# Low parts of weights by an accumulating SBUF transfer instead of a VectorE subtraction, in the middle of a hybrid decoder trunk

## The chip, the cores and the metric

The kernel runs on one core of a Trainium2 chip. A core has a matrix engine (TensorE, PE in the profile, with its weight loads shown apart as PEld), a vector engine (VectorE, DVE), an engine for pointwise functions (ScalarE, ACT), a programmable engine (GpSimd, POOL) and a queue engine (SyncE, SP). Data comes through 16 DMA engines, which SP, ACT and POOL can all start. The engines run side by side, each through its own instructions in order, and wait for each other by semaphores.

The metric is the device time of one execution in microseconds, as the median of the runs.

## The reference

Two layers, on 512 tokens of width 1024, all in float32. Each layer norms its input and projects it once into the inputs of three branches and three gates:

```python
xn = rmsnorm(x, norm1_g)
proj = xn @ w_in
...
y_ssd = ssd_mixer(...)          # Mamba-2: conv, chunked scan over 4 chunks of 128, gated norm
y_mla = mla_mixer(...)          # latent attention, 8 heads, causal
y_gdn = gdn_mixer(...)          # gated DeltaNet: conv, triangular solves, chunked scan
mixed = g_ssd * (y_ssd @ w_ssd_out) + g_mla * (y_mla @ w_mla_out) + g_gdn * (y_gdn @ w_gdn_out)
h = x + mixed @ w_out
f = jnp.square(jax.nn.relu(rmsnorm(h, norm2_g) @ w_up)) @ w_down
return h + f
```

The output is the norm of the second layer's result. Almost all of the arithmetic is in products of the 512 tokens with weight matrices that are read once.

## The kernel before

**Two-part arithmetic.** Every large product is made of three products of rounded numbers. A weight `w` is split into a high part, `w` rounded to the type float32r, and a low part, `w` minus the high part; activations likewise. `mm3` (L179) adds high x high, high x low and low x high in PSUM.

**How weights come in.** `weights` (L164) walks down a matrix. `weights_raw` (L157) loads 128 x 1024 float32 (512 KB) through SP's queue into a tile `wraw`, of which there are two buffers. Each such tile is split in two pieces of 128 x 512 by `split_half` (L148): ScalarE's copy rounds the piece into `whi` (L153), and VectorE subtracts it from the raw piece into `wlo` (L154). `whi` and `wlo` have four buffers each. `dense_F` (L185) and `dense_T` (L217) then issue twelve matmuls for each piece. A raw buffer can be loaded again when both of its pieces have been split; a `whi` or `wlo` buffer can be written again when the last matmul that reads it is done.

**The order of a layer.** First the small projections, the latents and attention (L353 to L660). Then, in a pool `br`, the part that the change concerns (L1038 to L1061): `ssd_group` twice (L685), each with projections, a convolution and a scan of four chunks; `gdn_decays` (L782), which loads and computes decay matrices and stores them; the output projection of attention, in two halves between these; `gdn_matrix` twice (L790) and `gdn_blocks` (L832), a chain of 62 small VectorE operations; the output projection of the state-space branch with the steps of `gdn_inverse` between its blocks; `gdn_unit` twice (L927), each with projections and a scan of four chunks; and the output projection of the gated-delta branch. `out_proj` (L462) also projects the gate of its branch. After that come `w_out` with the residual, and the feed-forward part.

**What sets the order.** A scheduler lays out each engine's instructions from the program and from priorities. The split of weights stands under a high priority, so that it goes ahead of other work on ScalarE and VectorE as soon as its buffers are free. POOL has little to do: it raises small tiles to the powers that norms need (`rsq`, L263, and L809, L939) and clears some tiles. The decay matrices `eE` are loaded through SP's queue, the same as the weights (L455, L820, L967).

Of the kernel before, what the change touches and what calls it, by code (L numbers as in the profile page):

```python
# [15 lines left out]
ALU = mybir.AluOpType  # L16
# [38 lines left out]
def hybrid_kernel(ctx, tc, a, out, depth=2, taps=None):  # L55
    nc = tc.nc
    pe, act, dve, pool, sync = nc.tensor, nc.scalar, nc.vector, nc.gpsimd, nc.sync
    uid = itertools.count()

    def mk(pl, shape, dt, tag, bufs=None):  # L60
        return pl.tile(shape, dt, tag=tag, name=f"{tag}_{next(uid)}", bufs=bufs)

    def tap(name, ap):
        if taps and name in taps:
            sync.dma_start(taps[name], ap)

    def f32(ap):
        return ap.bitcast(F32)
# [76 lines left out]
        act.activation(cosT, nn, AF.Sin)  # L145


    def split_half(raw, hold=None, first=True):  # L148

        n = raw.shape[1]  # L150
        hi, lo = hold or (mk(wp, [P, n], F32R, "whi"), mk(wp, [P, n], F32R, "wlo"))
        with tc.high_priority() if first else nullcontext():
            act.copy(hi, raw)  # L153
            dve.tensor_tensor(lo, raw, f32(hi), ALU.subtract)  # L154
        return hi, lo

    def weights_raw(w2d, c0, n, k0, kt):  # L157

        raw = mk(wp, [P, kt * n], F32, "wraw", 2)
        sync.dma_start(raw.rearrange("p (k n) -> p k n", n=n),  # L160
                       w2d[k0 * P : (k0 + kt) * P, c0 : c0 + n].rearrange("(k p) n -> p k n", p=P))
        return raw

    def weights(w2d, c0, n, K, hold=None, raw0=None):  # L164

        kt = min(1024 // n, K // P)
        step = 512 // n  # L170
        for k0 in range(0, K // P, kt):
            given = raw0 is not None and k0 == 0
            raw = raw0 if given else weights_raw(w2d, c0, n, k0, kt)
            for q in range(0, kt, step):
                hi, lo = split_half(raw[:, q * n : (q + step) * n], hold and hold[k0 + q], not given)
                v = lambda x: x.rearrange("p (k n) -> p k n", n=n)
                yield k0 + q, v(hi), v(lo)

# [6 lines left out]
    def dense_F(gen, cols, K, xh, xl, mid=None, banks=None, after=None):  # L185

        pss = banks or [acc_bank() for _ in cols]
        last = K // P - 1
        if mid:
            gen = list(gen)
            for i, hf in enumerate(HALVES):
                for ps, c in zip(pss, cols):
                    for k0, wh, wl in gen:
                        for k in range(wh.shape[1]):
                            kk = k0 + k  # L200
                            mm3(ps[:, hf], wh[:, k, c], wl[:, k, c], xh[kk][:, hf], xl[kk][:, hf], kk == 0, kk == last)
                if i == 0:
                    mid()
            return pss
        for k0, wh, wl in gen:
            for ps, c in zip(pss, cols):
                for k in range(wh.shape[1]):
                    a_, b_ = wh[:, k, c], wl[:, k, c]
                    mm3(ps[: a_.shape[1], :], a_, b_, xh[k0 + k], xl[k0 + k], k0 + k == 0, k0 + k == last)
            if after:  # L210
                after()
        return pss

    def tiles(n):
        return [slice(i, i + P) for i in range(0, n, P)]
# [55 lines left out]
    def hilo_tags(pl, base, n=KD, w=S):  # L271
        return ([mk(pl, [P, w], F32R, f"{base}h{k}") for k in range(n)],
                [mk(pl, [P, w], F32R, f"{base}l{k}") for k in range(n)])
# [44 lines left out]
    def small_weights(raw, first=True):  # L318
        res = []
        for q in range(2):  # L320
            hold = [mk(lp, [P, 384], F32R, "mix", 8) for _ in range(2)]
            hi, lo = split_half(raw[:, q * 384 : (q + 1) * 384], hold, first)
            res.append((4 * q, hi.rearrange("p (k n) -> p k n", k=4), lo.rearrange("p (k n) -> p k n", k=4)))
        return res
# [11 lines left out]
    for t in range(T):  # L336
        if t == 2:
            params = load_params(0, False)
        ss = mk(sp, [P, 2], F32, "nss", 4)
        for i in range(2):  # L340
            if t == 2 and i == 1:

                raws0 = small_raw(0), weights_raw(a["w_in"][0], O_CQ, 512, 0, 2)
            hf = slice(i * 512, (i + 1) * 512)
            sync.dma_start(xt[:, t, hf], xsrc[t * P : (t + 1) * P, hf])
            if t == i == 1:
                jk = mk(hpl, [P, 512], F32, "hj", 2)
                dve.scalar_tensor_tensor(jk, xt[:, t, hf], 1.0, xt[:, t, hf], ALU.mult, ALU.mult, accum_out=ss[:, i : i + 1])
            else:
                square(ss[:, i : i + 1], xt[:, t, hf], hpl, "hj")  # L350
        ssq.append(ss)
    xh, xl = hilo_tags(lp, "x")
    norm_half(0, [xt[:, t] for t in range(T)], ssq, lambda k: params[0][:, 124 + k : 125 + k], hpl, xh, xl)  # L353
    for ly in range(depth):
# [24 lines left out]
        smalls(HALVES[0])  # L379
        cq_tok = [mk(lp, [P, 512], F32, "mix", 8) for t in range(T)]  # L380
        dense_T(weights(w_in, O_CQ, 512, D, raw0=None if ly else raws0[1]), 512, D, xh, xl, lambda t, ps: act.copy(cq_tok[t], ps), mid=second_half)
        h_pool.close()

# [78 lines left out]
        def out_proj(w2d, br, yh, yl, pl, part=range(4), after=None):  # L462
            for dp in part:
                tg = []
                for ps in dense_F(weights(w_in, O_GATE + br * D + dp * 256, 256, D), tiles(256), D, xh, xl, after=after):
                    t_ = mk(pl, [P, S], F32, "cva", 2)
                    act.activation(t_, ps, AF.Tanh, scale=0.5)
                    tg.append(t_)
                for j, ps in enumerate(dense_F(weights(w2d, dp * 256, 256, D), tiles(256), D, yh, yl, after=after)):
                    d = 2 * dp + j  # L470
                    if mixed[d] is None:
                        mixed[d] = mk(lp, [P, S], F32, "mix", 8)
                        dve.scalar_tensor_tensor(mixed[d], tg[j], 1.0, ps, ALU.add, ALU.mult)
                    else:
                        dve.scalar_tensor_tensor(tg[j], tg[j], 1.0, ps, ALU.add, ALU.mult)
                        dve.tensor_tensor(mixed[d], mixed[d], tg[j], ALU.add)
# [57 lines left out]
        for hp in range(4):  # L534
# [67 lines left out]
            for j in range(2):  # L602
# [3 lines left out]
                for t in range(T):  # L606
                    n = max(256, (t + 1) * P)
# [9 lines left out]
                    n = (t + 1) * P  # L617
# [10 lines left out]
                for kbs in ((0,), (1,), (3, 2)):  # L628
                    ps = sm_bank()
                    n = 0  # L630
# [296 lines left out]
        def gdn_unit(u, kT, ork, cc, cd, Yt, yh, yl):  # L927
# [102 lines left out]
            for c in range(4):  # L1030
# [4 lines left out]
                split_gain(yh[k], yl[k], ps, col(g_gdn))  # L1035
                tap(f"ygdn{k}", f32(yh[k]))

        ys = hilo_tags(lp, "y")  # L1038
        d_e = mk(dr, [2, T, P, 4, P], F32, "d_e", 2)
        ssd_group(0, *ys)  # L1040
# [17 lines left out]
        for u in range(2):  # L1058
            gdn_unit(u, *mats[u], *yg)
        out_proj(a["w_gdn_out"][ly], 2, *yg, br)  # L1060
        bp.close()  # L1061


# [13 lines left out]
        with tc.tile_pool(name="wo", bufs=1, reuse_waits="tile") as wo:  # L1077
            for c in range(2):
# [6 lines left out]
                hold = list(zip(*hilo_tags(wo, "w"))) if c == 1 else None  # L1085
# [18 lines left out]
        with tc.tile_pool(name="ff", bufs=1, reuse_waits="tile") as fp:  # L1104
# [72 lines left out]
            def down(qd, ops, b):  # L1177
# [9 lines left out]
                def product(ps, n, raw, start, i, j, op, done):  # L1187

                    w = []
                    for k in range(4):  # L1190
                        w.append(split_half(raw(k)))
                        if done == 2 and qd == 3:
                            continue
                        for t in range(2):
                            mul(ps, n, w, k, t, start)
                    for t in range(2):
                        if done == 2 and qd == 3:
                            for k in range(4):
                                mul(ps, n, w, k, t, start)
                        r = 2 * i + t  # L1200
                        hs_ = h[:, r, j * 512 : (j + 1) * 512]
                        with tc.high_priority():
                            dve.tensor_tensor(hs_, hs_, ps[t], op)
                        if done and qd == 3:
                            square(h_ssq[r][:, j : j + 1], hs_, fp, "fs", 3)
                            if done == 2:
                                finish(r, gb)
# [82 lines left out]
```

## Time and profile before

| | |
|---|---|
| median of 2 runs | 2339.37 us (2336.67 to 2342.07) |
| profiled execution, its span | 2334.6 us; no other time is given for this execution, and the two runs shown lie 2.1 and 7.5 us above it |
| TensorE busy | 2294.8 us (98%), weight loads 1891.3 us (81%) |
| VectorE busy | 1582.1 us (68%) |
| ScalarE busy | 1159.8 us (50%) |
| GpSimd busy | 58.6 us (3%) |
| moved by DMA | 240.38 MB, mean 103 GB/s |

Busy time of TensorE counts pipelined matmuls from start to a modelled end, so a busy share near 100% says that it was never long without work, not that it ran at its peak. In a row of a group the form is: line, engine, operation, what is written and read, shapes, count, then busy time in total and the mean of one in nanoseconds, then the idle time of the engine just before these instructions and what ended most of it. A row of waits gives who waited for whom, the time in total, how often, and the longest. A row of DMA issues gives tile and source, the queue, the count, the size of one, and the median time in microseconds from the issue to the landing.

### The profile page before, as it was taken

The page shows a single profiled execution, that of the slowest core. Times are in us where ns is not written, and L with a number is a line of the kernel's source. Part 1 is how long each engine was busy: PE and PEld are TensorE (multiplying, and loading weights), DVE is VectorE, ACT ScalarE, POOL GpSimd, SP SyncE. Part 2 cuts the span into 40 slices and gives each one's busy share as a digit, 9 for nine tenths or more (in the row PEclk, how much of TensorE's full clock was granted, in tenths as well). Part 3 has the DMA queues.
Part 4 walks back from the last instruction along what each step waited for, and adds up shares of the span by engine and source line. Part 5 has one row for each costly group of instructions (what it writes and reads, how often), then busy time and mean ns, then how long its engine had stood idle before and what let it go on. Part 6 is the DMA issues. An engine that isn't in the chain of part 4 may idle for free.

```text
span 2334.6 us, 32156 instructions
## 1 busy us (share of the span) xinstructions
PE 2294.8 (98%) x11926; PEld 1891.3 (81%) x11926; DVE 1582.1 (68%) x3100; ACT 1159.8 (50%) x2403; POOL 58.6 (3%) x74
## 2 busy tenths in 40 slices
PE   8999999999999999999999999999999999999998
PEld 7788787878887888888888887888788878888886
DVE  6776656875675458668767765667756645677668
ACT  6656644333443345545656557443334434545545
POOL 0000000000000000000010000000000000000000
PEclk9999999999999999999999999999999999999999
DMA  4323533352222443243132235334422224333231
GB/s 136 87 63 92 169 101 109 109 154 73 86 69 72 140 150 108 73 127 108 44 101 81 82 91 170 101 105 139 118 82 86 68 77 158 126 118 100 91 109 46
DMA packets 208221, 240.38 MB, mean 103 GB/s; under 512 B 33920, under 2 KB 155456, under 8 KB 208064
## 3 DMA queue, kind: packets, MB, share of 16 engines
q1 hardware_dynamic: 204544, 233.07, 32.7%
q10 hardware_dynamic: 3520, 5.25, 0.9%
q8 instruction: 94, 1.54, 0.3%
q14 instruction: 63, 0.52, 0.1%
HBM read 221.41 MB, written 11.63 MB: 100 GB/s over the span
## 4 chain that ended last, share of the span: by engine, by line
PE 86%; DVE 7%; DMA 3%; ACT 2%; POOL 1%; issue 1%; ACTq 0%; SPq 0%; DVEq 0%; POOLq 0%
PE acc L181 22%; PE acc L182 22%; PE acc L183 22%; PE sm L183 2%; PE sm L182 2%; PE sm L181 2%; DVE wlo L154 1%; PE sm L730 1%; DMA eE<-d_c 1%; DVE tok L846 1%; DMA mix<-mix 1%; PE sm L633 1%; DVE gQ L845 1%; PE yt L182 1%; PE sm L1003 1%
## 5 line engine op out<-in xcount | busy, mean ns | idle before, releaser
L154 DVE TENSOR_TENSOR wlo<-wraw,whi 128x512 fp32r<-128x512 f32 x552 | 378.3, 689 | 429.2 <-ACT whi L153 412.4
L153 ACT CAST whi<-wraw 128x512 fp32r<-128x512 f32 x552 | 341.4, 621 | 598.0 <-PE acc L182 371.0
L183 PE MATMUL acc<-xh,wlo 128*128 128x512 f32 (+1 forms) x1184 | 460.9, 390 | 0.0
L181 PE MATMUL acc<-xh,whi 128*128 128x512 f32 (+1 forms) x1184 | 460.7, 390 | 0.0
L182 PE MATMUL acc<-xl,whi 128*128 128x512 f32 (+1 forms) x1184 | 460.0, 389 | 0.0
L183 PEld LDWEIGHTS acc<-xh,wlo 128*128 128x128 f32 x1184 | 223.6, 189 | 41.9
L182 PEld LDWEIGHTS acc<-xl,whi 128*128 128x128 f32 x1184 | 223.5, 189 | 42.0 <-DVE xl L261 0.4
L181 PEld LDWEIGHTS acc<-xh,whi 128*128 128x128 f32 x1184 | 223.2, 189 | 41.7 <-ACT xh L260 0.4
L181 PE MATMUL acc<-yh,whi 128*128 128x512 f32 x384 | 151.9, 399 | 0.0
L182 PE MATMUL acc<-yl,whi 128*128 128x512 f32 x384 | 151.4, 394 | 0.0
L183 PE MATMUL acc<-yh,wlo 128*128 128x512 f32 x384 | 151.3, 394 | 0.0
L183 PE MATMUL acc<-whi,xl 128*128 128x512 f32 (+1 forms) x384 | 144.0, 375 | 0.0
L182 PE MATMUL acc<-wlo,xh 128*128 128x512 f32 (+1 forms) x384 | 143.9, 375 | 0.0
L181 PE MATMUL acc<-whi,xh 128*128 128x512 f32 (+1 forms) x384 | 142.6, 374 | 0.0
L674 DVE SCALAR_TENSOR_TENSOR ckl<-acc,pc,ckl 128x511 f32<-128x511 f32 (+2 forms) x168 | 120.4, 744 | 16.9 <-ACT ckl L670 8.3
L153 ACT CAST whi<-wr 128x512 fp32r<-128x512 f32 x128 | 79.5, 621 | 68.2 <-PE acc L183 32.7
L183 PE MATMUL acc<-whi,yl 128*128 128x512 f32 x256 | 99.7, 389 | 0.0
L181 PE MATMUL acc<-whi,yh 128*128 128x512 f32 x256 | 99.7, 389 | 0.0
L182 PE MATMUL acc<-wlo,yh 128*128 128x512 f32 x256 | 99.6, 389 | 0.0
L154 DVE TENSOR_TENSOR wlo<-wr,whi 128x512 fp32r<-128x512 f32 x128 | 85.8, 686 | 12.5 <-ACT whi L153 11.7
L181 PEld LDWEIGHTS acc<-yh,whi 128*128 128x128 f32 x384 | 71.7, 188 | 16.8 <-ACT yh L260 1.7
L182 PEld LDWEIGHTS acc<-yl,whi 128*128 128x128 f32 x384 | 72.2, 188 | 15.3 <-issue 1.0
(411 smaller groups left out, 4545.3 us busy)
## 6 DMA issues: line engine op xcount, KB each, us to landing
wraw<-in_w_in_dram SPq DMA_DIRECT2D x148, 512.0 KB, 3.6
wraw<-in_w_up_dram SPq DMA_DIRECT2D x64, 512.0 KB, 3.6
wr<-in_w_down_dram SPq DMA_DIRECT2D x32, 1024.0 KB, 5.0
eE<-d_c SPq DMA_DIRECT2D x48, 256.0 KB, 4.0
wraw<-in_w_mla_out_dram SPq DMA_DIRECT2D x16, 512.0 KB, 3.4
eE<-d_e SPq DMA_DIRECT2D x32, 256.0 KB, 3.0
wraw<-in_w_ssd_out_dram SPq DMA_DIRECT2D x16, 512.0 KB, 3.4
wraw<-in_w_gdn_out_dram SPq DMA_DIRECT2D x16, 512.0 KB, 3.3
```

The costliest lines, as they stand in the source:

```text
L153: act.copy(hi, raw)
L154: dve.tensor_tensor(lo, raw, f32(hi), ALU.subtract)
L181: pe.matmul(o, ah, bh, start=start, stop=False, skip_group_check=more)
L182: pe.matmul(o, ah, bl, start=False, stop=False, skip_group_check=more)
L183: pe.matmul(o, al, bh, start=False, stop=stop, skip_group_check=more)
L633: pe.transpose(ps[:, n : n + P], pn[t][:, kb * P : (kb + 1) * P], ident)
L674: dve.scalar_tensor_tensor(acc[:, d:], ps[:, : S - d], taps_[3 - d], acc[:, d:], ALU.mult, ALU.add)
L730: pe.matmul(py[:, h * 64 : (h + 1) * 64], e2[h // 4][:, h % 4, :], xd[:, h * 64 : (h + 1) * 64], start=True, stop=True)
L845: dve.tensor_tensor(pd, bc_last(nb[:, m, m + 1 :], m + 1), bc_mid(xb[:, m, : m + 1], 31 - m), ALU.mult)
L846: dve.tensor_tensor(xb[:, m + 1 :, : m + 1], xb[:, m + 1 :, : m + 1], pd, ALU.add)
L1003: pe.matmul(po[:, h * P : (h + 1) * P], pt_[:, h, :], vn[:, h * P : (h + 1) * P], start=True, stop=True)
```

## The change

In the part of each layer from the first `ssd_group` to the last `out_proj`, `split_half` makes the low part in another way. ScalarE still copies the raw piece to `whi`. Then ScalarE multiplies the raw piece by minus one into `wlo`; since `wlo` is of type float32r this is minus the high part. Then POOL starts a transfer from the raw piece to `wlo` that adds what it brings to what is there: raw minus high. Outside that part the subtraction on VectorE stays. The flag `added` chooses, and is set and cleared in the layer's code.

```diff
-    def split_half(raw, hold=None, first=True):
+    def split_half(raw, hold=None, first=True, added=False):
...
         with tc.high_priority() if first else nullcontext():
             act.copy(hi, raw)
-            dve.tensor_tensor(lo, raw, f32(hi), ALU.subtract)
+            if added:
+                act.mul(lo, raw, -1.0)
+                pool.dma_start(out=lo, in_=raw, accum_op=ALU.add)
+            else:
+                dve.tensor_tensor(lo, raw, f32(hi), ALU.subtract)
         return hi, lo
...
+    added = [False]
...
-                hi, lo = split_half(raw[:, q * n : (q + step) * n], hold and hold[k0 + q], not given)
+                hi, lo = split_half(raw[:, q * n : (q + step) * n], hold and hold[k0 + q], not given, added[0])
...
+        added[0] = True
         ys = hilo_tags(lp, "y")
...
         out_proj(a["w_gdn_out"][ly], 2, *yg, br)
+        added[0] = False
         bp.close()
```

## The prediction

> **What bounds the kernel now.** I read the page first: busy shares, the chain that ended last, and the two groups that the change touches.
>
> ```profile
> span 2334.6 us, 32156 instructions
> ...
> PE 2294.8 (98%) x11926; PEld 1891.3 (81%) x11926; DVE 1582.1 (68%) x3100; ACT 1159.8 (50%) x2403; POOL 58.6 (3%) x74
> ...
> PE 86%; DVE 7%; DMA 3%; ACT 2%; POOL 1%; issue 1%; ACTq 0%; SPq 0%; DVEq 0%; POOLq 0%
> ...
> L154 DVE TENSOR_TENSOR wlo<-wraw,whi 128x512 fp32r<-128x512 f32 x552 | 378.3, 689 | 429.2 <-ACT whi L153 412.4
> L153 ACT CAST whi<-wraw 128x512 fp32r<-128x512 f32 x552 | 341.4, 621 | 598.0 <-PE acc L182 371.0
> ```
>
> TensorE carries 86% of the chain that ends last; VectorE carries 7%. The subtraction is the costliest VectorE group, yet VectorE waits 412.4 us for the high part ahead of it, and ScalarE waits 371.0 us for TensorE ahead of the high part. The weights are therefore prepared as soon as TensorE gives a buffer back, and TensorE is what everybody waits for.
>
> Next, the two stretches of the trace that the change covers (one per layer, from the first weights of the state-space group to the last of the gated-delta output), and a dense piece of the first. The columns are busy time and instructions of each engine, the granted clock, the mean busy share of the 16 DMA engines, and what they moved.
>
> ```profile
> core 0: us, PE busy (x) PEld busy (x) DVE busy (x) ACT busy (x) POOL busy (x), PEclk, DMA share, GB/s
> 165.00:785.00 620.00, 610.94 (x3314) 498.04 (x3315) 399.60 (x830) 278.40 (x593) 19.96 (x18) 0.99 0.36 102
> 1325.00:1940.00 615.00, 608.70 (x3326) 496.70 (x3325) 399.66 (x830) 279.96 (x596) 19.96 (x18) 1.00 0.35 103
> 740.00:780.00 40.00, 40.00 (x178) 33.14 (x177) 17.86 (x28) 11.21 (x19) 0.00 (x0) 1.00 0.37 106
> ```
>
> TensorE is idle 620 - 610.94 = 9.1 us and 615 - 608.70 = 6.3 us there: 15.4 us together. That is the whole prize, whatever VectorE is spared. The waits of TensorE in the first stretch say how much of it is VectorE's (time in total, times, longest):
>
> ```profile
> PE sm L730 <- DVE eE L725: 2.5, 2, 1.4
> PE sm L879 <- DMA wk<-d_x: 1.8, 1, 1.8
> PE sm L984 <- DVE tok L981: 1.7, 4, 0.5
> PE yt L1034 <- DVE tok L1029: 1.4, 2, 0.9
> PE sm L800 <- DVE ft L269: 0.8, 1, 0.8
> PE yt L763 <- DVE tok L758: 0.6, 1, 0.6
> ```
>
> VectorE: 7.0 us of 8.8. The same share of the second layer's 6.3 is about 5, so 12 us in both. None of these is a wait for weights.
>
> **The change part by part.** A piece is 512 columns of weights, and each feeds 12 matmuls. Per layer the two state-space groups have 20 pieces each, the three output projections 32 each, the two key tiles 4 each and the two gated-delta units 20 each: 184, so 368 in both layers.
>
> *Removed:* 368 x 0.689 = 254 us of VectorE, none of it in the list of TensorE's waits. VectorE falls from 400 to 273 of 620 us in a stretch. What it can give is some of the 12 us. Those waits are for the last link of short chains, not for a queue of subtractions, so I take a third: -4 us.
>
> *Added on ScalarE:* a multiplication by minus one of the same shape and rounding as the cast, so 368 x 0.621 = 229 us, 114 per layer: 278 becomes 393 of 620 us. It fits; what matters is its place in the weights' chain.
>
> *Added on POOL and the DMA engines:* 368 transfers of 128x512 f32 (256 KB), each waiting for its multiplication. The trace before has none from POOL and none that accumulates. Rows near it, with size and median time from issue to landing:
>
> ```profile
> eE<-d_c SPq DMA_DIRECT2D x48, 256.0 KB, 4.0
> d_e<-eE SPq DMA_DIRECT2D x16, 256.0 KB, 4.1
> mix<-mix ACTq DMA_DIRECT2D x16, 128.0 KB, 2.7
> h<-hd SPq DMA_DIRECT2D x4, 512.0 KB, 6.5
> out_dram<-h SPq DMA_DIRECT2D x8, 256.0 KB, 2.0
> ```
>
> Below: 2.0 us, a plain 256 KB out of SBUF at the quiet end. Above: 6.5 us, twice the bytes. Nearest is 4.1 us, a plain 256 KB out of SBUF in this very region. To add, the engine must read the destination as well as the source. The dense piece moves 106 GB/s at a share of 0.37, hence 286 GB/s when fully busy, so one more pass over 0.262 MB is 0.9 us. I take 4.1 + 0.9 = 5.0 us and keep 2.0 and 6.5.
>
> *Moved: when a raw buffer comes free.* There are two raw buffers of two pieces each, and SyncE loads a buffer again only when both low parts are made. The dense piece shows this, by start and duration, with the time to landing of its loads:
>
> ```profile
> 753.29 0.62 ACT L153 CAST whi<-wraw 128x512 fp32r<-128x512 f32 x1 [2.05 <-PE acc L182]
> ...
> 754.12 0.69 DVE L154 TENSOR_TENSOR wlo<-wraw,whi 128x512 fp32r<-128x512 f32 x1
> ...
> 754.84 0.37 SPq L160 DMA_DIRECT2D wraw<-in_w_gdn_out_dram  x1
> 756.01 0.62 ACT L153 CAST whi<-wraw 128x512 fp32r<-128x512 f32 x1 [2.10 <-PE acc L182]
> ```
> ```profile
> DMA to landing us min/median/max: 3.2/3.5/3.8
> ```
>
> The load goes out at 754.84, as the subtraction ends at 754.81. After the change it goes out when the accumulation has landed. A buffer's round is then: load 3.5, four operations on ScalarE 4 x 0.62 = 2.5, the second transfer L, hand-overs about 0.2; in sum 6.2 + L. TensorE runs 178 matmuls in 40 us, 0.225 us each, so it eats a piece in 2.70 us and the four pieces of both buffers in 10.8 us. **The transfer is hidden up to L = 4.6 us**; beyond, each four pieces cost L - 4.6. With the four low-part buffers there is more room (a piece has 3 x 2.70 = 8.1 us for 1.2 + L, so L up to 6.9), so the raw buffers decide. At L = 5.0 that is 0.4 us for each of 92 rounds, 37 us, if all ran at the dense pace; the mean pace of a stretch is 620/184 = 3.4 us a piece, so I count between two thirds and all: 25 to 37, **+31 us**.
>
> *DMA share.* With two passes a transfer takes 1.8 us of all 16 engines. In a stretch that is 0.36 x 620 + 184 x 1.8 = 554 of 620 us: it fits on average, not at the peak, where the decay matrices are loaded beside the weights:
>
> ```profile
> 275.00:330.00 55.00, 55.00 (x250) 45.47 (x250) 26.43 (x40) 32.13 (x68) 0.00 (x0) 1.00 0.48 144
> ```
> ```profile
> L153 ACT CAST whi<-wraw x19: 603/621/624, 277.4 to 327.8; 128x512 fp32r<-128x512 f32 x19
> ```
>
> 0.48 x 55 + 19 x 1.8 = 61 us in 55: +6 per layer, **+12 us**. In SyncE's queue the loads of decay matrices stand behind a waiting weight load and come later too; ScalarE, at 32 + 12 = 44 of 55 us, waits for them in order. That lies in these 12.
>
> *Moved past POOL:* powers for the norms share POOL's queue with the transfers:
>
> ```profile
> L265 POOL TENSOR_TENSOR gms<-gms,nhalf 128x4 f32<-128x4 f32 x8 | 9.3, 1163 | 148.7 <-DVE gms L264 128.8 <-DVE gss L937 19.9
> L939 POOL TENSOR_TENSOR grq<-gss,nhalf 128x8 f32<-128x8 f32 x2 | 3.3, 1674 | 108.0 <-DVE gss L937 108.0
> L809 POOL TENSOR_TENSOR gork<-gss,phalf 128x8 f32<-128x8 f32 x2 | 3.3, 1636 | 63.9 <-DVE gss L807 63.9
> L265 POOL TENSOR_TENSOR srs<-srs,nhalf 128x4 f32<-128x4 f32 x2 | 2.0, 1008 | 324.6 <-DVE srs L264 324.6
> ```
>
> These 14 per layer now hold up the transfer behind them while they wait for VectorE. At L = 5.0 a piece is 8.1 - 6.2 = 1.9 us early, enough for one power of 1.0 to 1.7 us, so I cost this at nothing; without that cover it is the third rival.
>
> A rule of the Trainium skill speaks against the change here (SBUF — State Buffer, "Who interferes with whom"): while VectorE runs a one-input operation in its two-port mode, GpSimd cannot write the descriptors of its own DMAs.
>
> ```profile
> L758 DVE TENSOR_SCALAR tok<-tok,srs 128x512 f32<-128x512 f32 x8 | 3.4, 482 | 1.7 <-POOL srs L265 1.7
> ```
>
> This is the operation meant: 482 ns against 689 for two inputs agrees with a faster mode; no run here shows the blocking. By the rule the sum would be at most 2 x 3.4 = 7 us higher; without it, as it stands.
>
> **Sum:** -4 + 31 + 12 = +39 us on the profiled span of 2334.6 us. The median of the runs shown, 2339.37, is 4.8 us above that span, and I keep the distance: 2334.6 + 39 + 4.8 = **2378 us**, 1.7% slower than the median.
>
> **The rivals.**
>
> *Hidden.* The transfer lands within 4.6 us, as the 2.0, 2.7, 4.0 and 4.1 us rows allow. TensorE never waits for weights; only the relief is left, 0 to 15 us: 2324 to 2339, say 2335. Against it: those rows are plain and from hardware queues. The Trainium skill (DMA: Bandwidth & Descriptors, "Anatomy of one DMA — SWDGE (gpsimd) path") gives a DMA from GpSimd 2.0 us plus its bytes at 436 GB/s: as an estimate 2.6 us here, 3.2 with a second read, which is this rival; no run here shows it.
>
> *The transfer becomes the bound (clearly slower).* Place: DMA engines and raw buffers. At L = 6.5 a round is 12.7 us, 1.9 too long, 92 times: 175 us, with the peak's 12, 2526. Or three passes, 2.75 us of all engines: 0.36 x 620 + 184 x 2.75 = 729 us in 620, +109 per layer, 2557. I put it at 2540. It decides from about L = 5.5. For it: two stages already sit at 0.48. Against: the stretches use only a third of the DMA time.
>
> *POOL's order.* If each of 28 powers costs TensorE 1.5 us: +42, 2381.
>
> That the change does not do what it says is no rival: the program after it has 368 more transfers on POOL and the subtractions gone.
>
> **How the numbers follow.** Forecast 0.42, its own range 2350 to 2425; hidden 0.27; bound by the transfer 0.25; POOL's order 0.05; an unforeseen large gain 0.01. The limit of 2% (about what a measurement of this kernel can tell from no change) is 2386. Same: all of hidden, 0.22 of the forecast, 0.03 of POOL's: 0.52. Slower: 0.20 + 0.25 + 0.02 = 0.47. Faster by 47 us is more than three times TensorE's idle time there: 0.01. The range goes from 2325 (all the relief) to 2540 (the middle of the second rival).
>
> **What would show it.** Right: TensorE idle before dense matmuls, released by the new transfers; SyncE's wait for the low part now on a POOL transfer; its time to landing near 5 us; a DMA share of 0.8 to 0.9 in the stretches. Hidden: stretches of 605 to 620 us with no such waits. Wrong upwards: a share near 1.0 and landings over 6 us. Outside the stretches nothing should move. What I rest on most, L and its passes, has no row of its own.

## The result, and the profile after

The changed kernel took **2454.24 us** (median of two runs, 2452.88 to 2455.61) against 2339.37: a ratio of 1.0502, 95% interval 1.0447 to 1.0558. It is 5.0% slower, 115 us, where the prediction said 39 us. Timed a second time beside experiments on another occasion, the same file gave 2456.66 against 2333.95 us: 1.0531 (1.0501 to 1.0561), 123 us.

The page of the changed kernel, the lines that answer to those of before: span, busy time, what the DMAs moved, the queue of the new transfers, the groups that the change touches, and the issues of DMAs (last column: median us from issue to landing). Lines behind L153 have moved by 4 to 8.

```profile
span 2453.8 us, 33089 instructions
...
PE 2328.6 (95%) x11926; PEld 1899.3 (77%) x11926; DVE 1356.0 (55%) x2732; ACT 1338.1 (55%) x2771; POOL 377.2 (15%) x442
...
DMA packets 261221, 336.93 MB, mean 137 GB/s; under 512 B 39808, under 2 KB 161344, under 8 KB 261056
...
q0 software_dynamic: 52992, 96.49, 22.4%
...
L153 ACT CAST whi<-wraw 128x512 fp32r<-128x512 f32 x552 | 339.0, 617 | 559.5 <-PE acc L188 194.9
L156 POOL DMA_DIRECT2D wlo<-wraw x368 | 319.8, 876 | 1140.3 <-ACT wlo L155 1019.5
...
L155 ACT ACTIVATE wlo<-wraw 128x512 fp32r<-128x512 f32 x368 | 230.5, 628 | 92.8 <-DMA wraw<-in_w_in_dram 51.8
...
L158 DVE TENSOR_TENSOR wlo<-wraw,whi 128x512 fp32r<-128x512 f32 x184 | 125.1, 689 | 151.8 <-ACT whi L153 151.5
...
wlo<-wraw POOLq DMA_DIRECT2D x368, 256.0 KB, 4.2
wraw<-in_w_in_dram SPq DMA_DIRECT2D x148, 512.0 KB, 4.1
```

The quantities of work are as foreseen. VectorE's subtraction of `wraw` went from 378.3 to 125.1 us, ScalarE's multiplication costs 230.5 us, and 368 transfers of 256 KB run on POOL's queue. The queue's 22.4% of 16 engines' span is 0.224 x 2453.8 / 368 = 1.49 us of all 16 engines for each transfer. TensorE executes the same 11926 matmuls, but is idle 2453.8 - 2328.6 = 125.2 us where it was idle 39.8, so 85 us more, and its busy time has grown by 34 us. The loads of `w_in`'s weights, untouched by the change, land in 4.1 us instead of 3.6 (medians).

Where the time lies shows in the same two stretches and in a dense piece (797 to 840 us) of the changed kernel; columns as for before.

```profile
core 0: us, PE busy (x) PEld busy (x) DVE busy (x) ACT busy (x) POOL busy (x), PEclk, DMA share, GB/s
165.00:850.00 685.00, 637.86 (x3363) 511.66 (x3364) 292.80 (x662) 372.19 (x788) 176.25 (x199) 0.98 0.72 163
1390.00:2060.00 670.00, 625.16 (x3320) 500.92 (x3318) 286.70 (x646) 366.38 (x774) 175.89 (x198) 0.99 0.72 164
797.00:840.00 43.00, 38.73 (x167) 30.74 (x166) 5.41 (x8) 16.32 (x30) 12.10 (x14) 1.00 0.80 167
```

The stretches, whose ends are rounded to 5 us, are 65 and 55 us longer. That is 120 together, about all of the 119 us by which the profiled span grew. In the dense piece, where TensorE was busy 40 of 40 us, it is busy 38.7 of 43. The waits of the changed kernel say for what (time in total, times, longest):

```profile
SPq L164 <- DMA wlo<-wraw: 1099.4, 179, 15.7
...
ACT whi L153 <- DMA wraw<-in_w_in_dram: 115.2, 40, 7.4
...
PEld acc L189 <- DMA wlo<-wraw: 55.6, 33, 4.2
...
PE acc L189 <- DMA wlo<-wraw: 42.0, 27, 3.7
```

TensorE now waits for low parts, and behind that ScalarE waits for raw tiles that are not loaded yet. SyncE's wait for the low part is on the transfer, as the prediction said it would be. The order of those waits is a circle: the transfer keeps the raw tile, the load waits for the raw tile, ScalarE for the load, the next transfer for ScalarE. Its period can be read from SyncE's queue. In the dense piece of each kernel each row is two loads, one for each raw buffer, so the distance between the starts of rows is one round of a buffer. Before:

```profile
749.28 5.93 SPq L160 DMA_DIRECT2D wraw<-in_w_gdn_out_dram  x2
760.11 5.81 SPq L160 DMA_DIRECT2D wraw<-in_w_in_dram  x2
770.98 5.98 SPq L160 DMA_DIRECT2D wraw<-in_w_gdn_out_dram  x2
```

After:

```profile
793.95 7.01 SPq L164 DMA_DIRECT2D wraw<-in_w_in_dram  x2
806.51 7.01 SPq L164 DMA_DIRECT2D wraw<-in_w_gdn_out_dram  x2
819.07 7.21 SPq L164 DMA_DIRECT2D wraw<-in_w_in_dram  x2
831.82 6.98 SPq L164 DMA_DIRECT2D wraw<-in_w_gdn_out_dram  x2
```

Before, 10.8 and 10.9 us, which is TensorE's own pace for four pieces. After, 12.6, 12.6 and 12.8: the circle sets the pace. The prediction had 6.2 + 5.0 = 11.2. One round of the changed kernel in ScalarE's and POOL's rows, from the load issued at 819.07:

```profile
823.40 0.62 ACT L153 CAST whi<-wraw 128x512 fp32r<-128x512 f32 x1 [2.45 <-DMA wraw<-in_w_in_dram]
823.92 0.62 ACT L155 ACTIVATE wlo<-wraw 128x512 fp32r<-128x512 f32 x1
824.46 0.60 ACT L153 CAST whi<-wraw 128x512 fp32r<-128x512 f32 x1
824.97 0.63 ACT L155 ACTIVATE wlo<-wraw 128x512 fp32r<-128x512 f32 x1
```
```profile
824.84 0.86 POOL L156 DMA_DIRECT2D wlo<-wraw  x1 [3.23 <-ACT wlo L155]
825.88 0.86 POOL L156 DMA_DIRECT2D wlo<-wraw  x1 [0.18 <-issue]
```

Load 819.07 to 823.40: 4.3 us. Four operations of ScalarE to 825.60: 2.2 us. From there to the next load of the buffer at 831.82: 6.2 us, of which 0.3 is the hand-over to POOL, which is still at work on the issue before, and 5.9 the transfer from the start of its issue to the freed buffer. Sum 12.7. In the trace this transfer lands 5.8 us after its issue; the load of the other buffer goes out at 825.90, just beside it.

### The profile page after: what moved, and what is told of

Same layout as the page of the kernel before. It is cut to its first block, busy times and chain, and to the rows that moved or that the text cites. A ratio compares the mean times of both kernels' runs of the same rounds, so it can differ in the third digit from the quotient of the medians.

```text
span 2453.8 us, 33089 instructions
## 1 busy us (share of the span) xinstructions
PE 2328.6 (95%) x11926; PEld 1899.3 (77%) x11926; DVE 1356.0 (55%) x2732; ACT 1338.1 (55%) x2771; POOL 377.2 (15%) x442
## 3 DMA queue, kind: packets, MB, share of 16 engines
q0 software_dynamic: 52992, 96.49, 22.4%
## 5 line engine op out<-in xcount | busy, mean ns | idle before, releaser
L153 ACT CAST whi<-wraw 128x512 fp32r<-128x512 f32 x552 | 339.0, 617 | 559.5 <-PE acc L188 194.9
L156 POOL DMA_DIRECT2D wlo<-wraw x368 | 319.8, 876 | 1140.3 <-ACT wlo L155 1019.5
L189 PE MATMUL acc<-xh,wlo 128*128 128x512 f32 (+1 forms) x1184 | 462.4, 391 | 22.5 <-DMA wlo<-wraw 22.4
L187 PE MATMUL acc<-xh,whi 128*128 128x512 f32 (+1 forms) x1184 | 464.6, 393 | 13.5 <-DVE tok L275 13.5
L155 ACT ACTIVATE wlo<-wraw 128x512 fp32r<-128x512 f32 x368 | 230.5, 628 | 92.8 <-DMA wraw<-in_w_in_dram 51.8
L158 DVE TENSOR_TENSOR wlo<-wraw,whi 128x512 fp32r<-128x512 f32 x184 | 125.1, 689 | 151.8 <-ACT whi L153 151.5
L680 DVE SCALAR_TENSOR_TENSOR ckl<-acc,pc,ckl 128x511 f32<-128x511 f32 (+1 forms) x168 | 122.3, 745 | 104.5 <-ACT ckl L678 60.6
L189 PE MATMUL acc<-yh,wlo 128*128 128x512 f32 x384 | 157.9, 411 | 19.6 <-DMA wlo<-wraw 19.6
L271 POOL TENSOR_TENSOR nrs<-nrs,nhalf 128x1 f32<-128x1 f32 x20 | 11.6, 583 | 789.8 <-DVE nrs L287 649.4
L153 ACT CAST whi<-wr 128x512 fp32r<-128x512 f32 x128 | 79.5, 621 | 68.3 <-PE acc L189 31.3
L189 PEld LDWEIGHTS acc<-yh,wlo 128*128 128x128 f32 x384 | 74.5, 194 | 42.0 <-DMA wlo<-wraw 26.5
```

The lines of the kernel that those rows point to most:

```text
L155: act.mul(lo, raw, -1.0)
L156: pool.dma_start(out=lo, in_=raw, accum_op=ALU.add)
L187: pe.matmul(o, ah, bh, start=start, stop=False, skip_group_check=more)
L189: pe.matmul(o, al, bh, start=False, stop=stop, skip_group_check=more)
L271: pool.tensor_tensor(o, o, (exp if exp is not None else nhalf)[:, : o.shape[1]], ALU.pow)
L680: dve.scalar_tensor_tensor(acc[:, d:], ps[:, : S - d], taps_[3 - d], acc[:, d:], ALU.mult, ALU.add)
```

## The experiments

Three theories stood at the start. **One:** the raw buffer is held until the accumulation lands, and the round of a raw buffer is then longer than TensorE needs for four pieces. **Two:** the transfers fill the DMA engines. **Three:** ScalarE's second operation for each piece delays its other work. Differences in microseconds are between medians of a run and of the kernel before on the same occasion; ratios have their 95% interval.

### A third raw buffer

```diff
-        raw = mk(wp, [P, kt * n], F32, "wraw", 2)
+        raw = mk(wp, [P, kt * n], F32, "wraw", 3)
```

The same at the two other places that make `wraw`; for room, the small tiles `mx` of attention go from 8 buffers to 7. Once on the changed kernel, once as a control on the kernel before.

> The changed kernel with three raw buffers in place of two; one of the eight buffers of the row maxima in attention is given up for the room. TensorE's order is that of the changed kernel. Theory one (a raw buffer is held until the accumulation has landed, and its round is too long): six pieces are 16.2 us of TensorE against a round of about 12.3, so most of the 115 us comes back: 2340 to 2375 us. Theory two (the transfers fill the 16 DMA engines, and all that passes through them is late): the bytes are the same, so 2430 us or more. Theory three (ScalarE's second operation for each piece): unchanged, 2430 us or more.

> The kernel before with the same third raw buffer, as the control. All theories: ScalarE waits 2 us in total for raw weights in the first stretch before, so nothing to gain: 2330 to 2342 us.

Measured: 2377.87 us on the changed kernel, 1.0188 (1.0166 to 1.0211), and 2342.40 on the kernel before, 1.0035 (1.0022 to 1.0049). The transfers, their bytes and TensorE's order stay as they are, and 79 of the 123 us go. The third buffer isn't worth anything by itself: on the kernel before, it costs 8 us together with the `mx` buffer given up for it. The waits of the run with three buffers:

```profile
PEld acc L189 <- DMA wlo<-wraw: 14.2, 10, 2.4
...
ACT whi L153 <- DMA wraw<-in_w_in_dram: 11.1, 4, 3.7
...
PE acc L189 <- DMA wlo<-wraw: 10.0, 9, 2.0
```

ScalarE's wait for the raw tiles of `w_in` falls from 115.2 to 11.1 us and TensorE's for low parts from 42.0 to 10.0. This speaks for theory one; 44 us stay.

### The transfer reads the high part, or DRAM, and leaves the raw buffer alone

```diff
-                pool.dma_start(out=lo, in_=raw, accum_op=ALU.add)
+                pool.dma_start(out=lo, in_=f32(hi), accum_op=ALU.add)
```

With the high part as source, the low parts of these weights become zero: the correction by low parts is left out of the result. The raw tile is free when ScalarE has read it, everything else stays. In the second run the source is the weight's own block in DRAM, so the result is the reference's, for 96 MB more from DRAM.

> The changed kernel, two raw buffers, with one word changed: the transfer adds the high part, not the raw piece, to minus the high part, so the low parts come out zero (the kernel leaves out the weights' low parts between attention and w_out). Same bytes, same multiplication, same queue, same wait of TensorE for the landing; only the raw buffer is free as soon as ScalarE has read it. Theory one (the raw buffer held until the landing): most of the loss that the third buffer brought back comes back here too, 2365 to 2400 us. Theory two (the DMA engines are full): 2440 us or more. The third buffer left 44 us over; those stay here under theory one, in the stage that loads the decay matrices.

> The changed kernel, but the accumulating transfer reads the piece from device memory, where the weights lie, not from the raw tile: the raw buffer is free when ScalarE has read it, at the same number of bytes through the DMA engines. Theory one: 2365 to 2410 us. Theory two: 2440 or more, since shorter rows (1 KB in most matrices) make the transfer dearer, not cheaper.

Measured: 2377.16 us, 1.0185 (1.0162 to 1.0209), and 2402.08, 1.0300 (1.0271 to 1.0328). Freeing the raw tile by another way gives the same 42 us as a third buffer. The hold is worth about **80 us** (123 less 42 to 44). Reading from DRAM frees the tile too, but costs 25 us more than reading SBUF: its transfers land in 5.5 instead of 4.9 us and its queue takes 27.6% of the DMA engines instead of 22.8%.

### ScalarE alone

```diff
                 act.mul(lo, raw, -1.0)
-                pool.dma_start(out=lo, in_=raw, accum_op=ALU.add)
+                dve.tensor_tensor(lo, raw, f32(hi), ALU.subtract)
```

> ScalarE's multiplication into the low tile stays, and VectorE's subtraction then writes over it; no transfer. ScalarE's 229 us and its place in the chain alone. If ScalarE is the cause of what is left over: 2365 to 2390 us. If not: 2330 to 2350.

Measured: 2339.92 us, 1.0023 (1.0012 to 1.0034). The 230 us of multiplications cost 5 us. Theory three falls as the main cause. (The scheduler lays out TensorE's work in another order here than in the changed kernel and in the kernel before, so the 5 us need not be ScalarE's alone.)

### The transfer beside the old subtraction: three runs that told little

VectorE's subtraction stays and makes the low part. Beside it, transfers go into one of four spare tiles that nobody reads: from the raw piece with a multiplication ahead (first), from the high part with a multiplication (second), from the high part without (third).

```diff
+                dve.tensor_tensor(lo, raw, f32(hi), ALU.subtract)
+                x = scr[next(turn) % len(scr)]
-                act.mul(lo, raw, -1.0)
-                pool.dma_start(out=lo, in_=raw, accum_op=ALU.add)
+                act.mul(x, raw, -1.0)
+                pool.dma_start(out=x, in_=raw, accum_op=ALU.add)
```

> VectorE's subtraction makes the low part again. Beside it, for each piece, ScalarE's multiplication and the accumulating transfer from the raw piece still run, but into a spare tile (one of four) that nobody reads. So the raw buffer is still held, the DMA engines and ScalarE carry the same, and TensorE does not wait for the transfer itself. Theory one: 2410 to 2460 us. Theory two: the same, 2410 to 2460. Theory three: the same. Were it the path through the low part itself (TensorE waiting for the transfer at the end of the chain), it would be 2335 to 2370.

> As the kernel beside it, but the spare transfer reads the high part, not the raw piece: the same bytes, the same multiplication, the same queue, and the raw buffer is free when the subtraction is done. Theory one: 2335 to 2375 us, some 70 us less than the kernel beside it. Theory two: no difference to it, 2410 to 2460. Theory three: no difference to it.

> VectorE's subtraction makes the low part; no second operation on ScalarE. Beside it, POOL accumulates the high part of each piece into one of four spare tiles that nobody reads: the traffic and POOL's queue alone. If the 44 us that the third raw buffer left over are the traffic: 2350 to 2380 us, with 8 to 14 us in each layer's stage of the decay matrices. If they are ScalarE's or the longer chain to the low part: 2330 to 2345.

Measured: 2575.43, 2640.69 and 2409.59 us; 1.1037 (1.1014 to 1.1060), 1.1321 (1.1284 to 1.1358), 1.0327 (1.0302 to 1.0351). None agrees with what was expected, and the second is 65 us slower than the first where theory one had it 70 us faster. As far as the rows show, the cause lies in the experiment. In the changed kernel a multiplication waits for a low-part buffer, which TensorE gives back at its pace. With spare tiles it waits only for the raw tile and for an older transfer; it takes its place in ScalarE's order and holds up the rounding of later pieces. The first run's row, where the change's multiplication waits 51.8 us:

```profile
ACT scr L157 <- DMA wraw<-in_w_in_dram: 216.3, 97, 8.2
```

In the third, the spare tiles lie in the pool `br`, whose space is attention's until attention is over, and some 30 of its 75 us arise there, at the head of the part in each layer. The first two are put aside; of the third only the size agrees with the next runs.

### What is left without the hold: bytes, second pass, queue

```diff
-                act.mul(lo, raw, -1.0)
-                pool.dma_start(out=lo, in_=raw, accum_op=ALU.add)
+                act.mul(lo, raw, 0.0)
+                pool.dma_start(out=lo, in_=f32(hi))
```

This is the plain copy from the high part. The others differ in the transfer alone: `out=lo[:, :16], in_=raw[:, :16], accum_op=ALU.add` is the narrow one, `out=lo, in_=raw` the plain copy that holds the raw tile, and `act.dma_start(out=f32(lo), in_=f32(hi))` the plain copy from ScalarE's queue.

> The changed kernel with the accumulating transfer cut to 16 of the 512 columns (8 KB instead of 256 KB) and the multiplication by 0 instead of minus 1, so that the low parts are left out of the result except for those columns. All 368 transfers, their waits on ScalarE, their place in GpSimd's queue and the hold of the raw buffer stay; the bytes go, and with them most of the time to landing. If what remains without the long hold (42 us with three raw buffers or with the high part as source) is traffic on the DMA engines and the time a transfer of 256 KB takes, then 2335 to 2350 us. If it is GpSimd's queue and the added hand-overs, 2370 us or more, with TensorE's waits on low parts still there.

> The changed kernel with the multiplication by 0 and a plain copy of the high part over the low part in place of the accumulating transfer (the low parts are then wrong: this leaves the subtraction out). The raw buffer is free as in the run that reads the high part (2377 us), the bytes are the same, only the second read of the destination is gone. If the residue of 42 us is traffic, the share of the DMA engines for these transfers falls by a third or more and the time to about 2350 to 2365 us; if it is GpSimd's queue and hand-overs, it stays at 2372 to 2382 us.

> The changed kernel with a plain copy of the raw piece over the low part in place of the accumulating transfer and the multiplication by 0 (the low parts are then wrong: this leaves the subtraction out). The raw buffer is held until the copy has landed, as in the change, and the order of TensorE's work is the same; only the accumulation is gone. It stands against the plain copy from the high part (2352 us), which holds nothing. If the hold costs because a round of load, two pieces on ScalarE and an accumulating transfer is longer than 10.8 us, a plain copy, about 1.2 us shorter, brings the round from 12.6 to about 11.2 us, and the hold costs 10 to 30 us instead of 77: 2360 to 2385 us. If any hold of the raw buffer by a transfer costs the 77 us, 2420 us or more. If the wait for the raw buffer is not the cause at all, 2352 us.

> The changed kernel with a plain copy of the high part over the low part issued by ScalarE's queue instead of GpSimd's accumulating transfer, and the multiplication by 0 (the low parts are then wrong: this leaves the subtraction out). GpSimd's queue has only the powers again. Against the same copy from GpSimd (2352 us, 18 above the kernel before): if GpSimd's order of powers and transfers is what is left there, 2332 to 2342 us; if it is ScalarE's second operation, the added latency and the order that the scheduler makes of it, 2345 us or more.

Measured:

| transfer | us | ratio | more than before, us |
|---|---|---|---|
| 8 KB, accumulating, holds raw | 2350.47 | 1.0071 (1.0054 to 1.0087) | 17 |
| 256 KB, plain, from the high part | 2352.36 | 1.0079 (1.0064 to 1.0094) | 18 |
| the same from ScalarE's queue | 2360.76 | 1.0108 (1.0092 to 1.0124) | 26 |
| 256 KB, plain, holds raw | 2364.88 | 1.0126 (1.0107 to 1.0145) | 30 |
| 256 KB, accumulating, from the high part (above) | 2377.16 | 1.0185 (1.0162 to 1.0209) | 42 |
| 256 KB, accumulating, holds raw: the change | 2456.66 | 1.0531 (1.0501 to 1.0561) | 123 |

The hold costs 80 us with the accumulating transfer and 30 - 18 = 12 with a plain one, whose run has the change's own order of TensorE's work. So the hold isn't dear by itself: its price follows the length of the transfer, as the prediction's round has it. The dense piece with the plain copy that holds the raw tile, in SyncE's queue, and its transfers:

```profile
754.23 5.43 SPq L164 DMA_DIRECT2D wraw<-in_w_in_dram  x2
764.59 5.70 SPq L164 DMA_DIRECT2D wraw<-in_w_gdn_out_dram  x2
775.32 6.95 SPq L164 DMA_DIRECT2D wraw<-in_w_in_dram  x2
786.23 5.77 SPq L164 DMA_DIRECT2D wraw<-in_w_gdn_out_dram  x2
```
```profile
wlo<-wraw POOLq DMA_DIRECT2D x16, 256.0 KB, 2.9
```

The rounds are 10.4, 10.7 and 10.9 us: TensorE's pace again, with transfers that land in 2.9 us where the accumulating ones of the change, in its dense piece, took this:

```profile
wlo<-wraw POOLq DMA_DIRECT2D x14, 256.0 KB, 5.2
```

The same bytes, the same source and destination, and 2.3 us between these medians. But a median hides here that a transfer's time depends on what runs beside it. Worked out from the traces of the two dense pieces, as start and time to landing in us:

```
plain copy that holds raw                  the change
load       764.59  3.95                    transfer   824.84  3.55
transfer   764.86  4.30                    transfer   825.88  5.80
transfer   767.52  2.27                    load       825.90  4.46
load       769.92  4.01                    load       831.82  3.97
transfer   770.22  4.35                    transfer   831.91  5.11
transfer   772.95  2.23                    transfer   832.95  5.35
```

A plain copy that goes out together with a load takes 4.3 us, one that goes out when the load has all but landed 2.3. The second transfer of a raw tile frees it. In the plain run that one comes late enough to have the engines nearly to itself; in the change it goes out together with the other buffer's load, or just behind it. The least times of the whole runs come near to what a transfer takes when undisturbed. In this order they are the change, the plain copy from the raw piece, and the plain copy from the high part, with 368 transfers each:

```profile
DMA to landing us min/median/max: 3.2/4.2/7.8
DMA to landing us min/median/max: 2.2/2.6/7.5
DMA to landing us min/median/max: 2.2/4.1/6.5
```

Transfers with no load and no other such transfer in flight beside them for over half a microsecond had medians of 3.24, 2.27 and 2.25 us (29, 59 and 23 of them, counted in the traces). So the accumulation by itself adds about 1 us, and 3.2 lies below the break-even of 4.6; the rest of the 5.8 comes with what runs beside it. This split is read from the traces; no run tests it alone.

Without a hold, the accumulation costs 42 - 18 = 24 us more than the plain copy. What stays with a plain copy, or with almost no bytes, is 17 to 18 us; by the run with ScalarE's multiplication alone, about 5 of these may be ScalarE's. Whether GpSimd's queue has a part in the rest stays open: with the copies on ScalarE's queue the time is 8 us longer, not shorter, but the scheduler lays out TensorE's work differently there, so this run is a weak witness.

### A fifth low-part buffer

```diff
-        hi, lo = hold or (mk(wp, [P, n], F32R, "whi"), mk(wp, [P, n], F32R, "wlo"))
+        hi, lo = hold or (mk(wp, [P, n], F32R, "whi"), mk(wp, [P, n], F32R, "wlo", 5))
```

This is on the kernel whose transfer reads the high part, with the same at the one other place that makes a low part, and `mx` again with 7 buffers. The question was whether the 24 us are low parts that come late.

> The run in which the transfer adds the high part instead of the raw piece (the low parts are zero, so the subtraction is left out; 2377 us, 42 above the kernel before), with five buffers for low parts instead of four. If TensorE waits there because a low part comes late (latency of the transfer), a fifth buffer gives it 2.7 us more: 2350 to 2365 us. If the DMA engines are too full in the stage with the decay matrices, or the order of the work costs, 2372 to 2382 us.

Measured: 2378.03 us, 1.0182 (1.0166 to 1.0198), the same as with four. This does not clear the late low parts, because the fifth buffer hardly gives them room. The transfer reads the high part, of which there are still four buffers, and ScalarE goes on waiting for TensorE to give one back; POOL now waits for that rounding:

```profile
ACT whi L153 <- PE acc L188: 231.9, 187, 3.9
```
```profile
POOL wlo L156 <- ACT whi L153: 819.7, 318, 9.0
```

TensorE's own waits for low parts are hardly shorter either, 13.3 us in total against 14.9, where the plain copy from the high part has 4.2: some 11 of the 24 us are booked as such waits. Besides, the `mx` buffer that is given up here was part of a control that cost 8 us. So late low parts, the fullness of the DMA engines and the order of the work all stay possible. The queue's share speaks for the second; this is its row with the plain copy, and then with the accumulating one, both from the high part:

```profile
q0 software_dynamic: 52992, 96.49, 12.9%
```
```profile
q0 software_dynamic: 52992, 96.49, 22.8%
```

That is 0.82 against 1.47 us of all 16 engines for each transfer. In the 60 us from 285 on, where the decay matrices come in, the share of the DMA engines is 0.77 with the plain and 0.90 with the accumulating transfer:

```profile
285.00:345.00 60.00, 58.17 (x260) 46.55 (x260) 17.96 (x25) 43.00 (x87) 10.49 (x20) 1.00 0.77 224
```
```profile
285.00:345.00 60.00, 56.77 (x242) 45.81 (x241) 13.85 (x20) 41.25 (x86) 16.33 (x19) 0.94 0.90 211
```

No run took the bytes of the decay matrices away, so this cause of the 24 us is argued from the rows and not shown by an experiment.

### Half of the pieces, and the change once more

```diff
-                hi, lo = split_half(..., not given, added[0])
+                hi, lo = split_half(..., not given, added[0] and q == 0)
```

Only the first piece of each raw tile is made by a transfer; VectorE subtracts for the second.

> The changed kernel with the accumulating transfer for the first piece of each raw buffer only; VectorE subtracts for the second. The first transfer then has a piece's time (2.7 us) more to land before its buffer is due, so by the hold of the raw buffer the round has no excess: theory one expects 2345 to 2370 us, what is left being half of the residue of 42 us and some late landings; if each transfer cost the same wherever it stands, half of 115 us: about 2395 us.

> The changed kernel once more, unaltered, beside the others on the same chip: 2450 to 2458 us, ratio 1.045 to 1.055 to the kernel before.

Measured: 2362.77 us, 1.0124 (1.0109 to 1.0140), and 2456.66, 1.0531 (1.0501 to 1.0561). Half of the transfers cost 29 us, a quarter of what all of them cost. That is what the hold theory expects, since the first has 2.7 us more to land; TensorE's order is another one in this run, so it is no proof by itself. It is the fastest of the versions that compute the reference's result with these transfers, and it is still slower than the kernel before. None of the runs beats that.

### Where each version loses

This table is worked out from the traces: the time between the first matmuls of neighbouring stages, less the same of before, in us (first layer / second layer).

```
stage                                     change       3 raw bufs   plain, holds  plain, high part
decay matrices, attention's output        21.6 / 17.5  11.3 / 13.7  14.1 / 12.7   8.2 /  6.5
second state-space group                   6.9 / 10.5  -1.3 / -0.4   0.4 /  0.2  -1.4 / -0.4
matrices, inverse, state-space output      7.0 /  8.6   0.1 /  5.9  -2.3 /  2.9  -5.3 / -1.1
gated-delta units                          7.8 /  7.8   1.9 /  1.9   0.9 /  1.2   1.8 /  3.3
gated-delta output, w_out                 10.9 / 12.8   2.4 /  2.3   2.1 /  2.1   2.1 /  2.0
all else                                   5.6 /  2.0   0.6 / -0.2  -2.4 / -2.7   0.8 / -0.8
```

With a third raw buffer the dense stages come back to within 2.4 us, and most of what is left lies where the decay matrices are loaded (another 6 us in the second layer's matrices). The 12 us that a hold costs with a plain copy lie there too, and so do nearly all of the 16 us that the plain copy from the high part costs by these traces.

## Why the prediction was right in kind and wrong in size

**What bounds the kernel** stood: TensorE's 15 idle us were the whole prize, and most of what happened came through the supply of weights. One after the other, the runs split the 123 us into about 80 for the hold with an accumulating transfer, 24 for accumulating without a hold, and 18 that a plain copy without a hold costs.

**Removed from VectorE, -4 us: not seen.** The 254 us went (378.3 to 125.1), but no run without a hold came out below the kernel before. In the changed kernel VectorE waits 125.6 us, in 8 waits, for `tok` from ScalarE (L274), a row that the kernel before does not have, and TensorE waits 13.5 us behind it. That the relief was lost there is argued, not shown: with a plain copy VectorE still waits over 100 us there, and TensorE no longer does.

**Added on ScalarE: right.** 229 us foreseen, 230.5 measured, and 5 us of time when it stands alone.

**The transfer: its parts nearly right.** 1.8 us of all engines foreseen, 1.49 measured; 5.0 us to landing foreseen, 4.2 in the median of all and 5.2 in the dense piece. A rule of the Trainium skill on which the hidden case leaned (DMA: Bandwidth & Descriptors, "Anatomy of one DMA — SWDGE (gpsimd) path") gives a plain transfer of this size 2.0 us plus its bytes at 436 GB/s, 2.6 as an estimate. The traces differ from it both ways: an undisturbed plain copy took 2.2 to 2.3, and the medians of the two runs with plain copies from POOL were 2.6 and 4.1, by what ran beside them, so the 2.6 agrees by chance. For the accumulating one the estimate with a second read at that rate, 3.2, is what an undisturbed one took; for the round it was too low by 1.0 in the median, 2.0 in the median of the dense piece and 2.6 for the transfer that frees the raw tile in the round shown. The share of the DMA engines in the stretches was 0.72, below the 0.8 to 0.9 foreseen.

**The round of the raw buffer, +31 us: the step that failed, by its size.** The place, the break-even and the queue were right; a plain copy, which lands below the 4.6 us, is hidden in the dense piece as the break-even says. But the term measured about 80 us. In the dense piece the round was 12.6 us, not 11.2: 1.8 over TensorE's 10.8 instead of 0.4. Two of its parts were too small. The load was kept at the 3.5 us that it took before, without such transfers beside it, and takes 4.3. The transfer with its hand-overs was set at 5.0 + 0.2, and is 6.2 from the end of the multiplication to the next load: 0.3 until POOL, which issues for 0.86 us each time, takes it up, 5.8 to the landing beside the other buffer's load, 0.1 to SyncE. The prediction gave the transfer one length; it has 3.2 alone and 5.8 in this place, one on each side of the break-even. ScalarE's four operations were a little shorter than set (2.2 for 2.5, as they overlap). The count of rounds went the other way: 80 us at 1.8 are 45 rounds of 92, half of them, where two thirds to all were counted. With the break-even only 0.4 us away, an error of 1.4 in a round of 11 made the excess of a round more than four times as large.

**The DMA share, +12 us: too small.** Accumulating instead of copying, without a hold, costs 24 us. No run shows that all of these are the DMA engines' fullness; late low parts may have a share. The stage named is where the table has most of what no hold explains, but how it divides was not settled.

**POOL's order, at nothing: not contradicted, and not shown.** In the changed kernel POOL waits 37.4 us, in 10 waits, for VectorE ahead of the powers of `gms`, and transfers behind them wait too; TensorE's share in that would be booked as a wait for the transfer. With the plain copy POOL waits as long, and by the table the gated-delta units cost 1.8 and 3.3 us. Moving the copies off POOL brought no gain, in another order of TensorE's work. The rule of the Trainium skill about VectorE's two-port mode (SBUF — State Buffer, "Who interferes with whom") would lengthen some issues of POOL. In the changed kernel they show 859 ns at the least, 859 in the median and 1669 at the most:

```profile
L156 POOL DMA_DIRECT2D wlo<-wraw x368: 859/859/1669, 144.7 to 2057.3; - x184
```

So at least half were not lengthened at all, and no run shows a cost of it. What lengthened the others stays open.

**Missing from the sum:** some 17 us that stay with a plain copy or with 8 KB. The multiplication may have 5 of them; for the rest no cause was shown. One rival has no run: between the kernel before and the changed one, 2283 of TensorE's 11926 matmuls stand at another place in its order (compared by tiles, from the traces), and the runs with 17 and 18 us keep the changed order.

**The rivals.** Hidden is what a plain copy in the dense piece did, not an accumulating one. The transfer as the bound was right about its place and gave L = 6.5 for it; with the hand-over of 0.2 that is 6.7 us to the next load where the forecast had 5.2. The measured 6.2 stands between the two, and so does the time.

## What to carry to other kernels

When an operation on a tile is replaced by a transfer, ask first how long its source is held: a buffer that was free after a 0.7 us operation is now busy until the landing, and the price is the excess of the whole round (load, operations, issue, transfer, hand-over back to the load) over the consumer's pace. Work that round out with the load and the transfer as they will be beside each other, not as either is alone, and when it comes within a microsecond of the pace, take the term as uncertain by its whole size. A source that is needed longer anyway, or one more buffer, brought two thirds of the loss back here. And engine time that nobody waits for, as that of VectorE's subtractions here, was worth nothing when it was freed.

## What the runs showed of the hardware beyond that

- **Accumulation costs POOL by the transfer, not by the byte, at the two sizes run.** The issue of an accumulating transfer keeps POOL for 859 ns with 256 KB, and for 862 in the run with 8 KB; a plain copy of 256 KB takes 530.

```profile
L156 POOL DMA_DIRECT2D wlo<-wraw x368: 862/862/1482, 142.7 to 1953.1; - x184
```
```profile
L156 POOL DMA_DIRECT2D wlo<-whi x368: 530/530/712, 144.9 to 1956.1; - x184
```

- **The second pass is a little less than a second pass.** An accumulating transfer takes 1.49 us of all engines against 0.82 to 0.83 for the plain copy, 1.8 times; to landing, 3.2 against 2.2 us at the least.
- **The granted clock fell where single waits of TensorE were long.** Where the decay matrices are loaded the granted clock, 1.00 before, was 0.91 in the changed kernel, with a wait of 3.7 us among TensorE's. In the dense piece, where TensorE was idle 4.3 of 43 us but in no wait longer than 1.6, it stayed at 1.00. Over the whole execution it went from 0.996 to 0.990; as an estimate, that is some 15 us (0.006 x 2454) of the 34 by which busy time grew. These are the stretch, its waits, and the waits of the dense piece:

```profile
290.00:346.00 56.00, 45.96 (x181) 35.47 (x180) 7.26 (x10) 31.88 (x70) 12.31 (x15) 0.91 0.82 193
```
```profile
PE acc L189 <- DMA wlo<-wraw: 8.8, 5, 3.7
```
```profile
PE acc L189 <- DMA wlo<-wraw: 4.2, 3, 1.6
```
